# Two trunk layers on one core: five of 22 tile pairs of the FFN's up projection by Strassen's scheme, and another place for the down projection's Strassen part

## The chip, the core and the metric

The kernel is one program on one core of a Trainium2 chip. TensorE (PE) multiplies matrices, with a second list (PEld) for loading the weights of the next matmul; VectorE (DVE) and ScalarE (ACT) do elementwise work and empty the accumulators; GpSimd (POOL) does little here; SyncE (SP) issues the DMAs. The metric is the device time of one execution in microseconds (us), lower is better, told as the median of several runs.

## The reference, cut to what matters

T = 528 tokens (16 learned meta tokens and 512 frames) of width 1024 go through two layers, each a mixer and a gated feed-forward net. Only the second half of a layer and the projection ahead of it matter here:

```python
for l in range(DEPTH):                       # DEPTH = 2
    h = h + hybrid_mixer(rms_norm(h, norm_mix[l]), ...)    # its last step: y @ w_out, 1024 x 1024
    n = rms_norm(h, norm_ffn[l])
    gate, up = split(n @ w_up[l], 2)         # w_up: 1024 x 5632, so 2816 columns each
    gate = causal_dwconv(gate, conv_ffn[l])  # per column, three tokens wide
    h = h + (silu(gate) * up) @ w_down[l]    # w_down: 2816 x 1024
return h[:, N_META:]
```

## The kernel before, in words

**Layout and precision.** Tokens lie on the free axis and features on the partitions, so an activation is a row of tiles of 128 features by 528 tokens, and a weight tile of 128x128 is what TensorE holds still while tokens stream through. Every fp32 product is made of three matmuls in the format float32r: each operand is a high part (its rounded copy) and a low part (the rest), and high·high, high·low and low·high add up in one PSUM accumulator. `stage()` (L230) loads a raw weight tile of up to 128x512, four inner tiles side by side, by a DMA on SP's queue into one of four buffers `wst`; `two()` (L235) makes `wh` (ScalarE, L241) and `wl` (VectorE, L242) of it, three buffers each. A raw tile is free again when its `wl` is there, a split tile when its matmuls are done. `spans()` (L245) cuts the tokens in two halves of 264; in the second layer, where the meta tokens' outputs are not needed, a gate tile has halves of 256 and 258 tokens and an up tile one stretch of 512. `denses()` (L252, matmul L267) makes output tiles over all inner tiles; `dense()` (L274) is the same for one tile.

**PSUM** has eight banks, in four pools of two, with the tags a, g, s and x.

**w_out** (loop at L982) makes four pairs of output tiles. For each tile VectorE adds the result to the residual (L993), SP stores `hk` to DRAM, and `Norm.feed` (L183) multiplies by the norm's gain and leaves X, high by ScalarE (L186) and low by VectorE (L187), and the running sum of squares. The norm's factor for each token, `rb`, is ready only a while later, so w_up works on X without it and multiplies its results by rb instead.

**w_up** (`ffn()`, loop at L1010) goes over 22 feature tiles j; each is a pair of output tiles, gate and up. The gate tile has banks "g" and "a" in turn (L1014), the up tile "s" and "a" (L1032). VectorE multiplies the gate halves by rb into `cs` (L1023); the convolution is one ScalarE step (L1026) and two VectorE steps (L1028) in `cv`; tanh (L1030) and L1031 give twice the silu; the up halves become `uu` (L1035), and L1036 multiplies both. The result F is split into high (ScalarE, L1063) and low (VectorE, L1064) for w_down. For the first eight j, `parts()` (L1042 to L1061) instead forms the operands of a Strassen scheme, of two neighbouring feature tiles and two token halves: four blocks in the tile's own buffer, three more in `far`, a buffer with the tag "ar".

**w_down** (loop at L1074) makes four pairs of output tiles. A pair of output tiles, two inner tiles and two token halves are a 2x2 block product, which in Winograd's form of Strassen's scheme takes seven block products in place of eight. Each output pair begins with this for the first eight feature tiles: raw tiles (L1097), sums of weight blocks `s12` and `s34` on VectorE (L1106 to L1109), and the products (matmul L1091). Two products share a bank X1 or X2 (tag x) with others, so the sums P1, U2, U3, U4 of products are taken in between (L1125, L1138 to L1144). Then the other 14 feature tiles follow in chunks of four (L1146), with `addto` (L1134) adding the Strassen sums to the residual after the first of them.

**Order.** The program is written in the order above; the Tile framework's scheduler sets the order of the instructions on each engine by it, with the splits and weight sums raised to the front (`tc.high_priority(HI)`), and inserts the semaphores.

## Time and profile before

| | |
|---|---|
| runs, us | 1706.68, 1707.40, 1707.92; median 1707.4 |
| profiled execution, us | 1708.38, its span 1706.5 |
| granted TensorE clock | 0.999 |
| DMA | 173.78 MB, 102 GB/s over the span |
| w_out, layer 0 / layer 1 | 437.0 to 485.4 / 1290.0 to 1337.8 |
| w_up, layer 0 / layer 1 (without its first gate tile) | 493.5 to 740.1 / 1345.6 to 1583.6 |
| w_down, layer 0 / layer 1 | 740.1 to 864.7 / 1583.6 to 1706 |

The stages are stretches of the one profiled execution, in us from the span's start, cut where TensorE goes over to the next. In the views, "busy" is an engine's time at work, "x" a count of instructions, a line like `L242 DVE TENSOR_TENSOR wl<-wst,wh` an operation by its place in the code with the tiles that it writes and reads, and "<-" behind a wait the engine and instruction that ended it. A granted clock of 1.00 is full speed.

### The profile page before, as it was taken

The numbers are of one execution on the slowest core, as the hardware profiler recorded it, in microseconds if no ns is written. First come the engines' busy times: TensorE is split into PE (matmuls) and PEld (weight loads), VectorE is DVE, ScalarE is ACT, GpSimd is POOL, SyncE is SP. The second block draws the span as 40 slices with busy tenths as digits, with TensorE's granted clock in tenths as the row PEclk, the third lists the DMA queues.
The fourth block names the chain that finished last, engine by engine and source line by source line (L and its number), as shares of the span: only waits on it lengthen the run. The fifth ranks groups of instructions, "written<-read, shape, count | busy, mean of one in ns | idle before, by whom it ended". The sixth has DMA issues, their size and how long they took to land.

```text
span 1706.5 us, 34827 instructions
## 1 busy us (share of the span) xinstructions
PE 1695.2 (99%) x13476; PEld 1586.5 (93%) x13476; DVE 1281.4 (75%) x2998; ACT 777.8 (46%) x1697; POOL 75.2 (4%) x190
## 2 busy tenths in 40 slices
PE   9999999999999999999999999999999999999999
PEld 8899888889999999999998999888899999999888
DVE  6899999866667766666558998998666677666654
ACT  6553566653444433334335535566634444333332
POOL 1000111100000000000000000110000000000000
PEclk9999999999999999999999999999999999999999
DMA  6322211225533222234343122112265333333433
GB/s 206 99 63 87 76 51 46 83 72 178 173 116 90 93 88 93 89 108 144 117 141 99 62 88 81 51 45 80 70 180 175 113 94 96 93 93 95 130 118 100
DMA packets 95094, 173.78 MB, mean 102 GB/s; under 512 B 10704, under 2 KB 15536, under 8 KB 94672
## 3 DMA queue, kind: packets, MB, share of 16 engines
q1 hardware_dynamic: 93456, 167.01, 32.0%
q10 hardware_dynamic: 1472, 4.54, 0.8%
q8 instruction: 106, 1.74, 0.4%
q14 instruction: 60, 0.49, 0.1%
HBM read 154.04 MB, written 17.06 MB: 100 GB/s over the span
## 4 chain that ended last, share of the span: by engine, by line
PE 91%; DVE 5%; ACT 2%; issue 1%; DMA 0%; ACTq 0%; DVEq 0%
PE a L267 62%; PE a L1091 13%; PE misc L303 2%; PE iq L303 2%; PE vps L740 1%; PE oBT L903 1%; PE isc L486 1%; PE tps L751 1%; PE logit L879 1%; DVE wl L242 1%; PE PTp L897 1%; PE dS L794 0%; ACT ar L789 0%; ACT junk L656 0%; DVE va L777 0%
## 5 line engine op out<-in xcount | busy, mean ns | idle before, releaser
L267 PE MATMUL a<-X,wh 128*128 128x264 f32 (+4 forms) x4768 | 947.4, 295 | 0.0
L267 PEld LDWEIGHTS a<-X,wh 128*128 128x128 f32 x4768 | 755.1, 188 | 20.3 <-issue 0.2
L267 PE MATMUL a<-X,wl 128*128 128x264 f32 (+4 forms) x2384 | 701.2, 294 | 0.0
L241 ACT ACTIVATE wh<-wst 128x512 fp32r<-128x512 f32 (+2 forms) x512 | 313.7, 613 | 603.2 <-PE a L267 329.4
L242 DVE TENSOR_TENSOR wl<-wst,wh 128x512 fp32r<-128x512 f32 (+2 forms) x512 | 341.7, 668 | 178.9 <-ACT wh L241 163.3
L267 PEld LDWEIGHTS a<-X,wl 128*128 128x128 f32 x2384 | 450.0, 189 | 10.9
L1091 PE MATMUL a<-F,wh 128*128 128x264 f32 (+2 forms) x984 | 202.5, 303 | 0.0
L1091 PEld LDWEIGHTS a<-F,wh 128*128 128x128 f32 x984 | 157.7, 188 | 7.8
L1091 PE MATMUL a<-F,wl 128*128 128x264 f32 (+2 forms) x492 | 149.0, 303 | 0.6 <-DVE wl L242 0.6
L1091 PEld LDWEIGHTS a<-F,wl 128*128 128x128 f32 x492 | 92.6, 188 | 4.8 <-DVE wl L242 1.0
L267 PE MATMUL a<-Y,wh 128*128 128x264 f32 (+2 forms) x512 | 92.9, 283 | 0.0
L267 PEld LDWEIGHTS a<-Y,wh 128*128 128x128 f32 x512 | 79.1, 188 | 0.0
L267 PE MATMUL a<-Y,wl 128*128 128x264 f32 (+2 forms) x256 | 72.5, 283 | 0.0
L1028 DVE SCALAR_TENSOR_TENSOR cv<-cs,vec,cv 128x528 f32<-128x528 f32 (+1 forms) x88 | 67.0, 761 | 3.1 <-ACT cv L1026 1.1
L1023 DVE TENSOR_TENSOR cs<-a,rb 128x264 f32<-128x264 f32 (+1 forms) x88 | 37.4, 427 | 38.8 <-PE a L267 35.8
L1035 DVE TENSOR_TENSOR uu<-a,rb 128x264 f32<-128x264 f32 (+1 forms) x66 | 33.9, 516 | 32.6 <-PE a L267 32.6
L361 DVE SCALAR_TENSOR_TENSOR cv<-cs,vec,cv 128x528 f32<-128x528 f32 x72 | 54.3, 756 | 0.9 <-ACT cv L359 0.8
L844 DVE MAX8 m<-ar 128x8 f32<-128x256 f32 (+2 forms) x96 | 53.1, 553 | 1.1
L845 DVE MATCH_REPLACE8 ar<-m,ar 128x256 f32<-128x256 f32 (+2 forms) x96 | 51.8, 540 | 0.0
L267 PEld LDWEIGHTS a<-Y,wl 128*128 128x128 f32 x256 | 48.2, 188 | 0.0
L1030 ACT ACTIVATE th<-cv 128x528 f32<-128x528 f32 (+1 forms) x44 | 27.8, 633 | 31.8 <-DVE cv L1028 31.7
L1031 DVE SCALAR_TENSOR_TENSOR cv<-th,cv 128x528 f32<-128x528 f32 (+1 forms) x44 | 30.7, 698 | 13.8 <-ACT th L1030 13.7
(352 smaller groups left out, 2458.0 us busy)
## 6 DMA issues: line engine op xcount, KB each, us to landing
wst<-w_up SPq DMA_DIRECT2D x176, 256.0 KB, 2.7
wst<-w_down SPq DMA_DIRECT2D x80, 256.0 KB, 2.7
wst<-w_a SPq DMA_DIRECT2D x64, 256.0 KB, 2.7
wst<-w_gate SPq DMA_DIRECT2D x64, 256.0 KB, 2.9
wst<-w_out SPq DMA_DIRECT2D x32, 256.0 KB, 2.9
hk<-h SPq DMA_DIRECT2D x24, 264.0 KB, 3.4
tg<-gg SPq DMA_DIRECT2D x16, 264.0 KB, 2.3
gr<-tg SPq DMA_DIRECT2D x16, 264.0 KB, 2.7
```

The source lines that it names most:

```text
L241: S.activation(h, w, AF.Copy)
L242: V.tensor_tensor(lo, w, h.bitcast(F32), op=sub)
L267: mms.append(PE.matmul(ps[j][:, :t.stop - t.start], w[:, ws], x[:, t], start=(kk == 0 and w is h and part == 0), stop=(kk == kts - 1 and w ...
L303: mms.append(PE.matmul(b[:, c:], X[kk][:, part, o:o + 128], w[:, c:], start=(kk == 0 and w is h and part == 0), stop=(kk == KT - 1 and w i ...
L361: V.scalar_tensor_tensor(cv, cs[:, i:i + T], vc(cw + i), cv, op0=mul, op1=add)
L844: V.max(m8, sc)
L845: V.match_replace(sc, m8, sc, SEL)
L1023: V.tensor_tensor(cs[:, 2 + t.start:2 + t.stop], p, rb[:, t], op=mul)
L1028: V.scalar_tensor_tensor(cv[:, t0:], cs[:, t0 + i:i + T], vec[:, cw + i:cw + i + 1], cv[:, t0:], op0=mul, op1=add)
L1031: V.scalar_tensor_tensor(cv[:, t0:], th[:, t0:], 1.0, cv[:, t0:], op0=add, op1=mul)
L1035: V.tensor_tensor(uu[:, t], p, rb[:, t], op=mul)
L1091: PE.matmul(o, c(ww), r, start=first, stop=fin and ww is w[1], skip_group_check=True)
```

## The change

Three things change.

- **w_up.** For the five feature tiles j in `UP` the gate tile and the up tile are made together, by the scheme that w_down uses: the two output tiles, neighbouring inner tiles and two token halves as blocks, over the whole inner dimension of eight tiles. `up7()` does it. The scheme itself is the new function `seven()` (L277 of the changed kernel), which both projections call. A pair has two raw tiles for each half of the inner dimension, hence all four `wst` buffers, eight weight sums in `wsum`, and 84 matmuls (L284) of half the tokens. The three steps one, mid and end add up the products in `cs` and `uu`, and the multiplications by rb follow there as two instructions of the full width. The remaining 17 pairs stay as they were.
- **w_out.** What the scheme needs of X beside its blocks (T1 to T4, high and low) is formed behind each pair of output tiles, by six VectorE instructions of half the tokens and one of all, and ScalarE's high parts. Three of the four sets lie in the buffer "ar", the fourth in the buffer of feature tiles 20 and 21.
- **w_down.** The Strassen scheme now takes the last eight feature tiles in place of the first eight, so that `far` is filled after w_up's use of "ar" is over. For the first output pair the three plain chunks of four come first, then Strassen, then the addition to the residual and the last chunk of two; the other output pairs begin with Strassen as before.

The number of matmuls stays the same, and their columns fall from 3,268,590 to 3,237,990. The diff, cut to its core (w_down's old lines, which do the same as `seven()`, are left out):

```diff
@@ -27,6 +27,7 @@
 SP = 4
 INV = -2e38
+UP = (2, 5, 8, 11, 14)
@@ -273,6 +274,49 @@
+    def seven(src, ks, ops, sums, X1, X2, C0, C1, C2, first, steps):
+        def mm3(o, st, w, c, x):
+            for ww, part in ((w[0], 0), (w[0], 1), (w[1], 0)):
+                PE.matmul(o, ww[:, c:c + 128], x[:, part], start=st, stop=False, skip_group_check=True)
+                st = False
+        def run(jobs, w, i, stride, off):
+            for o, res, name, blk in jobs:
+                for q in range(2):
+                    mm3(o, first(res) if i == 0 and q == 0 else False, w, off * blk + stride * q, ops[2 * i + q][name])
+        raw, ss, wa = [], [], []
+        for k in ks:
+            r = [stage(src[u][:, k * 128:k * 128 + 512], 512).rearrange("p (q c) -> p q c", q=2) for u in range(2)]
+            raw.append(r)
+            wa.append(two(r[0].rearrange("p q c -> p (q c)"), 512))
+        for i, r in enumerate(raw):
+            t12, t34 = [t.rearrange("p (a q c) -> p a q c", a=2, q=2) for t in sums(i)]
+            A = [r[i // 2][:, :, 128 * (i % 2):128 * (i % 2) + 128] for i in range(4)]
+            with tc.high_priority(HI):
+                V.tensor_tensor(t12[:, 0], A[2], A[3], op=add)
+                V.tensor_tensor(t34[:, 0], A[0], A[2], op=sub)
+                V.tensor_tensor(t12[:, 1], t12[:, 0], A[0], op=sub)
+                V.tensor_tensor(t34[:, 1], A[1], t12[:, 1], op=sub)
+            ss.append([t.rearrange("p a q c -> p (a q c)") for t in (t12, t34)])
+        n = range(len(ks))
+        for i in n:
+            run([(X1, "X1", "B11", 0), (C0, 0, "B21", 1)], wa[i], i, 256, 128)
+        steps[0]()
+        for i in n:
+            w = [t.rearrange("p q c -> p (q c)") for t in two(raw[i][1][:, :, 128:], 256)]
+            run([(C2, 2, "T4", 0)], w, i, 128, 0)
+        for i in n:
+            run([(X2, "X2", "T2", 1), (X1, "X1", "T1", 0)], two(ss[i][0], 512), i, 128, 256)
+        steps[1]()
+        for i in n:
+            run([(C1, 1, "B22", 1), (X2, None, "T3", 0)], two(ss[i][1], 512), i, 128, 256)
+        steps[2]()
@@ -979,6 +1023,11 @@
+        nh = (T - t0 + 3) // 4 * 2
+        s1, s2 = slice(t0, t0 + nh), slice(T - nh, T)
+        xar = p1.tile([128, AR], F32R, tag="ar", name="xar")
+        xq = None
+        nf.ops = []
@@ -995,6 +1044,29 @@
+            i = m0 // 2
+            if i == 3:
+                xq = Q(10, [128, 2112], F32R, name="xq")
+            tv = (xq if i == 3 else xar[:, 8 * nh * i:])[:, :8 * nh].rearrange("p (a b t) -> p a b t", a=4, b=2)
+            e, o = hks
+            ge, go = [gains[:, nf.off + m0 + u:nf.off + m0 + u + 1] for u in range(2)]
+            td = p2.tile([128, T], F32, tag="cv", name="td", bufs=2)
+            tt = p2.tile([128, T + 3], F32, tag="cs", name="tt", bufs=2)
+            d, f, t3, t2 = td[:, :nh], td[:, nh:2 * nh], tt[:, :nh], tt[:, nh:2 * nh]
+            S.activation(f, e[:, s2], AF.Copy, scale=ge)
+            V.tensor_tensor(d, e[:, s2], e[:, s1], op=sub)
+            V.scalar_tensor_tensor(t3, o[:, s2], go, f, op0=mul, op1=sub)
+            V.scalar_tensor_tensor(t2, e[:, s1], ge, t3, op0=mul, op1=add)
+            S.activation(tv[:, 0, 0], d, AF.Copy, scale=ge)
+            V.scalar_tensor_tensor(tv[:, 0, 1], d, ge, tv[:, 0, 0].bitcast(F32), op0=mul, op1=sub)
+            V.scalar_tensor_tensor(f, o[:, s1], go, t2, op0=mul, op1=sub)
+            for k, x in ((slice(1, 3), tt[:, :2 * nh].rearrange("p (a t) -> p a t", a=2)), (slice(3, 4), f[:, None])):
+                S.activation(tv[:, k, 0], x, AF.Copy)
+                V.tensor_tensor(tv[:, k, 1], x, tv[:, k, 0].bitcast(F32), op=sub)
+            xe, xo = nf.x[m0:m0 + 2]
+            nf.ops.append(dict(B11=xe[:, :, s1], B21=xo[:, :, s1], B22=xo[:, :, s2],
+                               T1=tv[:, 0], T3=tv[:, 1], T2=tv[:, 2], T4=tv[:, 3]))
@@ -1006,12 +1078,45 @@
-        far = p1.tile([128, AR], F32R, tag="ar", name="far")
+        mh = (T - t0 + 3) // 4 * 2
+        z1, z2 = slice(t0, t0 + mh), slice(T - mh, T)
+        J0 = FT - 2 * SP
+        def up7(j, cs, uu):
+            g = "ga"[j % 2]
+            b0, b1 = [sm([128, mh], "a", g) for _ in range(2)]
+            b2 = sm([128, mh], "a", "s")
+            X1, X2 = [sm([128, mh], "a", "x") for _ in range(2)]
+            pu = p1.tile([128, 1024], F32, tag="ikT", name="pu")
+            P1, U2, U3 = [pu[:, mh * i:mh * i + mh] for i in range(3)]
+            sq = p1.tile([128, 2112], F32, tag="Q9", name="wsum")
+            c1, c2 = [cs[:, 2 + z.start:2 + z.stop] for z in (z1, z2)]
+            def one():
+                S.activation(P1, X1, AF.Copy)
+                V.tensor_tensor(c1, b0, P1, op=add)
+            def mid():
+                V.tensor_tensor(U2, X2, P1, op=add)
+                V.tensor_tensor(c2, X1, U2, op=add)
+            def end():
+                V.tensor_tensor(U3, X2, P1, op=add)
+                V.tensor_tensor(c2, c2, b1, op=add)
+                V.tensor_tensor(uu[:, z1], b2, U3, op=add)
+                V.tensor_tensor(uu[:, z2], X1, U3, op=add)
+            seven([a["w_up"][l, 2 * j + u] for u in range(2)], (0, 4), nf.ops,
+                  lambda i: [sq[:, 1024 * i + 512 * u:1024 * i + 512 * u + 512] for u in range(2)],
+                  X1, X2, b0, b1, b2, lambda i: True if i is not None else False, (one, mid, end))
         for j in range(FT):
+            if j == J0:
+                far = p1.tile([128, AR], F32R, tag="ar", name="far")
 ...
-            ps = dense(a["w_up"][l, 2 * j], KT, lambda k, part: X[k][:, part], t0, "ga"[j % 2])
+            ps = None if j in UP else dense(a["w_up"][l, 2 * j], KT, lambda k, part: X[k][:, part], t0, "ga"[j % 2])
 ...
-            for p, t in ps:
-                V.tensor_tensor(cs[:, 2 + t.start:2 + t.stop], p, rb[:, t], op=mul)
+            if j in UP:
+                uu = p2.tile([128, T], F32, tag="hk", name="uu", bufs=2)
+                up7(j, cs, uu)
+                V.tensor_tensor(cs[:, 2 + t0:2 + T], cs[:, 2 + t0:2 + T], rb[:, t0:], op=mul)
+            else:
+                for p, t in ps:
+                    V.tensor_tensor(cs[:, 2 + t.start:2 + t.stop], p, rb[:, t], op=mul)
 ...
-            ps = pu0 if j == 0 else dense(a["w_up"][l, 2 * j + 1], KT, lambda k, part: X[k][:, part], t1, "sa"[j % 2])
-            uu = p2.tile([128, T], F32, tag="hk", name="uu", bufs=2)
-            for p, t in ps:
-                V.tensor_tensor(uu[:, t], p, rb[:, t], op=mul)
+            if j in UP:
+                V.tensor_tensor(uu[:, t1:], uu[:, t1:], rb[:, t1:], op=mul)
+            else:
+                ps = pu0 if j == 0 else dense(a["w_up"][l, 2 * j + 1], KT, lambda k, part: X[k][:, part], t1, "sa"[j % 2])
+                uu = p2.tile([128, T], F32, tag="hk", name="uu", bufs=2)
+                for p, t in ps:
+                    V.tensor_tensor(uu[:, t], p, rb[:, t], op=mul)
             V.tensor_tensor(uu[:, t1:], uu[:, t1:], cv[:, t1:], op=mul)
-            if j < 2 * SP:
+            if j >= J0:
                 ys = yt[:, :8 * nh].rearrange("p (a b t) -> p a b t", a=4, b=2)
-                ye = far[:, 6 * nh * (j // 2):6 * nh * (j // 2 + 1)].rearrange("p (a b t) -> p a b t", a=3, b=2)
+                ye = far[:, 6 * nh * ((j - J0) // 2):6 * nh * ((j - J0) // 2 + 1)].rearrange("p (a b t) -> p a b t", a=3, b=2)
 ...
+            def strassen():
+                tt = p2.tile([128, T], F32, tag="th", name="ts", bufs=2)
+                tu = p2.tile([128, T], F32, tag="th", name="tu", bufs=2)
+                P1, U2, U3, U4 = tt[:, :nh], tt[:, nh:2 * nh], tu[:, :nh], tu[:, nh:2 * nh]
+                def one():
+                    S.activation(P1, X1, AF.Copy)
+                def mid():
+                    V.tensor_tensor(U2, X2, P1, op=add)
+                    V.tensor_tensor(U4, X1, U2, op=add)
+                def end():
+                    V.tensor_tensor(U3, X2, P1, op=add)
+                    V.tensor_tensor(U2, X1, U3, op=add)
+                def sums(i):
+                    return (p2.tile([128, T + 3], F32, tag="cs", name="s12", bufs=2)[:, :512],
+                            p2.tile([128, T], F32, tag="cv", name="s34", bufs=2)[:, :512])
+                seven(src, range(J0, FT, 4), S7, sums, X1, X2, C[0], C[1], C[2], first, (one, mid, end))
+                return P1, U4, U3, U2
+            def others(k0):
+                kn = min(WC, J0 - k0)
                 for u in range(2):
                     w = weights(src[u][:, k0 * 128:(k0 + kn) * 128], kn * 128)
+                    for h in range(1 if wide else 2):
+                        o = cb[u][:, :2 * nh] if wide else C[2 * u + h]
+                        t = slice(t1, T) if wide else (s1, s2)[h]
                         for k in range(kn):
+                            for ww, part in ((w[0], 0), (w[0], 1), (w[1], 0)):
+                                PE.matmul(o, ww[:, 128 * k:128 * k + 128], Yf[k0 + k][:, part, t],
+                                          start=first(2 * u + h) if k == 0 and part == 0 and ww is w[0] else False,
+                                          stop=False, skip_group_check=True)
+            ks = list(range(0, J0, WC))
+            n = len(ks) - 1 if m0 == 0 else 0
+            for k0 in ks[:n]:
+                others(k0)
```

More of the change, by code (lines that the diff above doesn't have):

```diff
@@ L1084, in ffn @@
             C = [cb[i // 2][:, nh * (i % 2):nh * (i % 2 + 1)] if wide else cb[i][:, :nh] for i in range(4)]
-            new = [True] * 4
             X1, X2 = [sm([128, nh], "a", "x") for _ in range(2)]
-            def mm3(o, first, w, c, x, t=None, fin=False):
-                for ww, part in ((w[0], 0), (w[0], 1), (w[1], 0)):
-                    r = x[:, part] if t is None else x[:, part, t]
-                    PE.matmul(o, c(ww), r, start=first, stop=fin and ww is w[1], skip_group_check=True)
-                    first = False
@@ L1095, in ffn @@
-            pairs = range(0, SP, 2)
-            raw, s12, s34, wa = [], [], [], []
-            for p0 in pairs:
-                r = [stage(src[u][:, p0 * 256:p0 * 256 + 512], 512).rearrange("p (q c) -> p q c", q=2) for u in range(2)]
-                raw.append(r)
-                wa.append(two(r[0].rearrange("p q c -> p (q c)"), 512))
-            for r in raw:
-                t12 = p2.tile([128, T + 3], F32, tag="cs", name="s12", bufs=2)[:, :512].rearrange("p (a q c) -> p a q c", a=2, q=2)
-                t34 = p2.tile([128, T], F32, tag="cv", name="s34", bufs=2)[:, :512].rearrange("p (a q c) -> p a q c", a=2, q=2)
-                A = [r[i // 2][:, :, 128 * (i % 2):128 * (i % 2) + 128] for i in range(4)]
-                with tc.high_priority(HI):
-                    V.tensor_tensor(t12[:, 0], A[2], A[3], op=add)
-                    V.tensor_tensor(t34[:, 0], A[0], A[2], op=sub)
-                    V.tensor_tensor(t12[:, 1], t12[:, 0], A[0], op=sub)
-                    V.tensor_tensor(t34[:, 1], A[1], t12[:, 1], op=sub)
-                s12.append(t12.rearrange("p a q c -> p (a q c)"))
-                s34.append(t34.rearrange("p a q c -> p (a q c)"))
@@ L1112, in ffn @@
-            cols = lambda o: (lambda w: w[:, o:o + 128])
-            def run(jobs, w, p0, i, stride, off):
-                for o, first, name, blk in jobs:
-                    for q in range(2):
-                        mm3(o, first and i == 0 and q == 0, w, cols(off * blk + stride * q), S7[p0 + q][name])
-            for i, p0 in enumerate(pairs):
-                run([(X1, True, "B11", 0), (C[0], True, "B21", 1)], wa[i], p0, i, 256, 128)
-            tt = p2.tile([128, T], F32, tag="th", name="ts", bufs=2)
@@ L1123, in ffn @@
-            tu = p2.tile([128, T], F32, tag="th", name="tu", bufs=2)
-            P1, U2, U3, U4 = tt[:, :nh], tt[:, nh:2 * nh], tu[:, :nh], tu[:, nh:2 * nh]
-            S.activation(P1, X1, AF.Copy)
-            for i, p0 in enumerate(pairs):
-                w = two(raw[i][1][:, :, 128:], 256)
-                w = [t.rearrange("p q c -> p (q c)") for t in w]
-                run([(C[2], True, "T4", 0)], w, p0, i, 128, 0)
-            for i, p0 in enumerate(pairs):
-                w = two(s12[i], 512)
-                run([(X2, True, "T2", 1), (X1, True, "T1", 0)], w, p0, i, 128, 256)
+            begun = set()
@@ L1134, in addto, with first @@
+            def first(i):
+                if i is None or i in ("X1", "X2"):
+                    return i is not None
+                b = i // 2 if wide else i
+                r = b not in begun
+                begun.add(b)
+                return r
             def addto(i, x):
@@ L1136, in addto @@
                 V.scalar_tensor_tensor(d, x, 0.5, d, op0=mul, op1=add)
-            V.tensor_tensor(U2, X2, P1, op=add)
-            V.tensor_tensor(U4, X1, U2, op=add)
-            for i, p0 in enumerate(pairs):
-                w = two(s34[i], 512)
-                run([(C[1], not wide, "B22", 1), (X2, False, "T3", 0)], w, p0, i, 128, 256)
-            V.tensor_tensor(U3, X2, P1, op=add)
-            V.tensor_tensor(U2, X1, U3, op=add)
-            for k0 in range(2 * SP, FT, WC):
-                if k0 == 2 * SP + WC:
-                    for i, x in enumerate((P1, U4, U3, U2)):
-                        addto(i, x)
-                kn = min(WC, FT - k0)
+            def strassen():
[15 more added lines that the diff above has]
+                return P1, U4, U3, U2
@@ L1162, in ffn @@
+            ks = list(range(0, J0, WC))
+            n = len(ks) - 1 if m0 == 0 else 0
+            for k0 in ks[:n]:
+                others(k0)
+            us = strassen()
+            for i, k0 in enumerate(ks[n:]):
+                if i == 1 or m0 == 0:
+                    for c, x in enumerate(us):
+                        addto(c, x)
+                others(k0)
             for u in range(2):
```

8 lines of the change are left out of this document (removed).

## The prediction

> **What bounds the kernel now.** The page comes first, for the share of each engine and for the chain.
>
> ```profile
> span 1706.5 us, 34827 instructions
> ...
> PE 1695.2 (99%) x13476; PEld 1586.5 (93%) x13476; DVE 1281.4 (75%) x2998; ACT 777.8 (46%) x1697; POOL 75.2 (4%) x190
> ...
> PE 91%; DVE 5%; ACT 2%; issue 1%; DMA 0%; ACTq 0%; DVEq 0%
> ```
>
> TensorE is busy for 99% of the span and holds 91% of the chain, so time goes only where matmul columns go, and it comes back where TensorE starts to wait. Whether it can wait is read stage by stage, from the windows: w_out of layer 0, w_up of layer 0, four of its plain pairs of tiles, the second Strassen pair of w_down in layer 0, and w_up of layer 1.
>
> ```profile
> core 0: us, PE busy (x) PEld busy (x) DVE busy (x) ACT busy (x) POOL busy (x), PEclk, DMA share, GB/s
> 437.00:485.40 48.40, 48.40 (x400) 48.40 (x400) 27.87 (x48) 19.70 (x33) 0.00 (x0) 1.00 0.54 169
> 493.50:740.10 246.60, 246.60 (x2018) 246.60 (x2018) 180.05 (x313) 98.39 (x163) 1.99 (x20) 1.00 0.30 91
> 587.30:634.20 46.90, 46.90 (x386) 46.90 (x385) 31.56 (x52) 17.71 (x28) 0.40 (x4) 1.00 0.30 91
> 768.50:784.00 15.50, 15.40 (x126) 15.13 (x125) 13.94 (x30) 8.15 (x15) 0.00 (x0) 1.00 0.58 174
> 1345.60:1583.60 238.00, 238.00 (x1514) 215.65 (x1514) 173.50 (x291) 97.71 (x163) 1.99 (x20) 1.00 0.31 94
> ```
>
> In w_up TensorE has no gap; VectorE (DVE) is at 73% in both layers, ScalarE at 40%. The fourth row matters most: a Strassen pair with VectorE at 90% of the time, and TensorE still at 15.40 of 15.50 us. The waits view gives what TensorE loses to splits of weights in the whole program, three times in all, in w_down:
>
> ```profile
> PE a L1091 <- DVE wl L242: 1.2, 3, 0.6
> ```
>
> **The matmuls.** Layer 0: 246.60 us over 2018 matmuls of 264 columns is 122.2 ns each. A plain pair is 2 tiles x 8 inner tiles x 2 halves x 3 = 96; by Strassen it is 7 products x 4 x 3 = 84. So 12 x 122.2 ns = 1.47 us less a pair, 7.3 us for five. Layer 1: a plain pair is 48 matmuls of 256 or 258 columns and 24 of 512, 24,624 columns in all; the window holds 21 pairs, so 238.0 / 21 = 11.33 us a pair, 0.460 ns a column. After it, 84 x 258 = 21,672 columns, 9.97 us; 1.36 us less, taken at 1.34 because 258-column matmuls might cost a little more by the column, 6.7 us for five. Together **14.0 us**. The seven products are in the order of the changed program, so this much is certain to leave TensorE's list. The clock is 1.00 in every window.
>
> **What VectorE gets.** Its prices, layer 0, w_up:
>
> ```profile
> L242 DVE TENSOR_TENSOR wl<-wst,wh 128x512 fp32r<-128x512 f32 x84 | 57.9, 689 | 12.2 <-ACT wh L241 12.0
> L1028 DVE SCALAR_TENSOR_TENSOR cv<-cs,vec,cv 128x528 f32<-128x528 f32 x44 | 33.8, 769 | 1.5 <-ACT cv L1026 0.3
> L1023 DVE TENSOR_TENSOR cs<-a,rb 128x264 f32<-128x264 f32 x44 | 18.9, 431 | 19.8 <-PE a L267 19.4 <-ACT rb L221 0.2
> L1031 DVE SCALAR_TENSOR_TENSOR cv<-th,cv 128x528 f32<-128x528 f32 x22 | 15.6, 708 | 13.7 <-ACT th L1030 13.5
> L1036 DVE TENSOR_TENSOR uu<-uu,cv 128x528 f32<-128x528 f32 x21 | 14.7, 700 | 0.0
> L1106 DVE TENSOR_TENSOR s<-wst 128x256 f32<-128x256 f32 x2 | 0.8, 421 | 0.0
> ```
>
> A plain pair: 4 splits of 0.69, 4 evacuations of 0.43, two steps of 0.77, then 0.71, 0.70 and a last split of 0.70: 8.1 us (7.9 measured, 31.56 / 4). A Strassen pair: 6 splits of 0.69 and 2 of 0.42, 8 weight sums of 0.42, 7 steps on the products of 0.43, 2 multiplications by rb of 0.70, and the same 3.65 of convolution, gate and split: 16.4 us. Every third pair is a Strassen pair, so three pairs hold 32.7 us of VectorE against 2 x 11.73 + 10.27 = 33.7 us of TensorE. At these whole durations VectorE is nearly the bound. But they overlap:
>
> ```profile
> 506.38 0.70 DVE L1036 TENSOR_TENSOR uu<-uu,cv 128x528 f32<-128x528 f32 x1
> 507.12 0.43 DVE L1055 TENSOR_TENSOR uu<-uu 128x264 f32<-128x264 f32 x1
> ...
> 603.62 0.43 DVE L1023 TENSOR_TENSOR cs<-a,rb 128x264 f32<-128x264 f32 x1 [0.20 <-PE a L267]
> ...
> 768.54 0.42 DVE L1106 TENSOR_TENSOR s<-wst 128x256 f32<-128x256 f32 x1 [2.76 <-DMA wst<-w_down]
> 768.88 0.68 DVE L242 TENSOR_TENSOR wl<-wst,wh 128x512 fp32r<-128x512 f32 x1
> 769.48 0.42 DVE L1107 TENSOR_TENSOR s<-wst 128x256 f32<-128x256 f32 x1
> 769.82 0.42 DVE L1108 TENSOR_TENSOR s<-s,wst 128x256 f32<-128x256 f32 x1
> ```
>
> An instruction that doesn't read the one ahead starts 0.08 us before that one's end: 0.34 us after a start of 256 columns, 0.60 after one of 512 (so 0.35 for 264, 0.63 for 528, 0.68 for a 0.77 step). One that reads it starts 0.04 after the end (506.38 to 507.12). With that, a queue of VectorE work is a tenth shorter, some 30 us in three pairs. [...]
>
> **The tightest place.** VectorE's list at a plain pair, program before (names: cs, uu the evacuated tiles, wl the low split, F the operand for w_down):
>
> ```order
> L242 TENSOR_TENSOR wl<-wst,wh 128x512
> L1023 TENSOR_TENSOR cs<-a,rb 128x264 x2
> L242 TENSOR_TENSOR wl<-wst,wh 128x512
> L1028 SCALAR_TENSOR_TENSOR cv<-cs,vec_158,cv 128x528 x2
> L1031 SCALAR_TENSOR_TENSOR cv<-th,cv 128x528
> L242 TENSOR_TENSOR wl<-wst,wh 128x512
> L1035 TENSOR_TENSOR uu<-a,rb 128x264 x2
> L242 TENSOR_TENSOR wl<-wst,wh 128x512
> L1036 TENSOR_TENSOR uu<-uu,cv 128x528
> ```
>
> And after, where Strassen pair 11 begins while pair 10 is still being finished:
>
> ```order
> L305 TENSOR_TENSOR wsum<-wst,wsum 128x256
> L1138 SCALAR_TENSOR_TENSOR cv<-cs,vec_158,cv 128x528
> L243 TENSOR_TENSOR wl<-wst,wh 128x512
> L1148 TENSOR_TENSOR uu<-a,rb 128x264
> L1141 SCALAR_TENSOR_TENSOR cv<-th,cv 128x528
> L1148 TENSOR_TENSOR uu<-a,rb 128x264
> L243 TENSOR_TENSOR wl<-wst,wh 128x256
> L1149 TENSOR_TENSOR uu<-uu,cv 128x528
> L243 TENSOR_TENSOR wl<-wst,wh 128x256
> L1177 TENSOR_TENSOR F_7958<-uu,F_7958 128x528
> L1097 TENSOR_TENSOR cs<-a,pu 128x264
> L243 TENSOR_TENSOR wl<-wsum,wh 128x512 x4
> ```
>
> The first weight sum's split stands behind the whole end of the pair before it, and the four raw tiles take all four staging buffers. Their DMA and ScalarE's part:
>
> ```profile
> wst<-w_up SPq DMA_DIRECT2D x176, 256.0 KB, 2.7
> ```
>
> ```profile
> L241 ACT ACTIVATE wh<-wst 128x512 fp32r<-128x512 f32 x83 | 52.1, 628 | 85.5 <-PE a L267 51.9 <-issue 33.5
> ...
> L1063 ACT ACTIVATE F<-uu 128x528 fp32r<-128x528 f32 x13 | 8.4, 646 | 17.9 <-DVE uu L1036 17.9
> ```
>
> Zero is the pair's first matmul. The fourth raw tile's buffer comes free with the second split of pair 10's up tile, about -6.7; 2.7 us of DMA and the issue put it at -3.7. From there: three sums 1.10, a cv step 0.68, a sum 0.34, a cv step 0.77, a split 0.61, uu 0.35, the gate product 0.68, uu 0.35, a split of 256 0.34, product 0.63, split 0.34: +2.4. F waits for ScalarE (0.65), starts at 2.9 and takes 0.63; the evacuation of the first product 0.35; the split 0.61: **+4.5**. TensorE wants it at the third matmul after 36, 36 x 0.122 + 0.245 = 4.65. It fits by 0.15 us. The other nine pairs have the same list (layer 1 with 0.2). I take 0.1 us of wait a pair for scatter, 1.0 in all; the ends are 0 and 1.0 us each. Behind an even Strassen pair the next tile needs its gate banks back at 5.87 and 7.34 us after the pair; VectorE's list gets there at 5.6 and 7.1. At the first odd tile, pair 1 of layer 0, the sums of pair 2 push the second bank's evacuation to 9.9 us after that tile's start against 9.5: 0.4 us.
>
> **w_down.** Its work is the same, but in the first output pair Strassen now stands behind three chunks, and only 24 matmuls (2.9 us) part it from that of the second pair; before it was 168 (20.5 us). VectorE there, before (X the next layer's operands, s_ the sums):
>
> ```order
> L1109 TENSOR_TENSOR s_10009<-wst,s_10008 128x256
> L1136 SCALAR_TENSOR_TENSOR hk<-a,hk 128x264
> L242 TENSOR_TENSOR wl<-wst,wh 128x256
> L1136 SCALAR_TENSOR_TENSOR hk<-a,hk 128x264 x2
> L187 SCALAR_TENSOR_TENSOR X_9962<-hk,gains,X_9962 128x528
> L242 TENSOR_TENSOR wl<-wst,wh 128x256
> L187 SCALAR_TENSOR_TENSOR X_9970<-hk,gains,X_9970 128x528
> L242 TENSOR_TENSOR wl<-s_10002,wh 128x512
> ```
>
> and after:
>
> ```order
> L305 TENSOR_TENSOR s_10170<-wst,s_10169 128x256
> L1211 SCALAR_TENSOR_TENSOR hk<-ts,hk 128x264
> L1211 SCALAR_TENSOR_TENSOR hk<-a,hk 128x264
> L243 TENSOR_TENSOR wl<-wst,wh 128x256
> L1211 SCALAR_TENSOR_TENSOR hk<-a,hk 128x264 x3
> L188 SCALAR_TENSOR_TENSOR X_10121<-hk,gains,X_10121 128x528
> L243 TENSOR_TENSOR wl<-s_10163,wh 128x512
> ```
>
> The residual additions of the first pair's Strassen results have joined the queue ahead of the first sum's split. Walked as above it ends 5.3 us into the second pair's Strassen, against 4.65: 0.7, where before 768.50 to 784.00 lost 0.1 and the waits 0.6 at most; the first pair loses 0.3 at the step that frees its second product. I charge 1.1 us for both layers, with -0.4 (the old waits go) and 2.5 as ends.
>
> **w_out and the rest.** Forming the new operands adds, for each of four output pairs, six VectorE instructions of 264 (0.35) and one of 528 (0.63), 2.7 us, and 1.9 of ScalarE. In layer 0 VectorE goes from 27.87 to 38.8 of 48.4 us, 80%; the free fifth covers it, and the last X7 is ready at 3.3 us of the first gate tile, which wants it at 4.0. Without that cover 2.7 us would fall on the path; I take 0.5 for both layers (0 to 2). Moving w_down's operand work from the first eight feature tiles to the last eight moves a load that cost TensorE nothing.
>
> **Sum.** -14.0 + 1.0 + 0.4 + 1.1 + 0.5 = -11.0 us. The profiled execution took 1708.4 us (span 1706.5 and 1.9 around it), 1.0 above the median of the runs, 1707.4. So 1697.4 there, and **1696.4** for the median.
>
> **Rivals.**
> *Nothing waits* (0.14): the window with VectorE at 90% speaks for it, the margin of 0.15 us against it. -14.0: 1693.4.
> *VectorE pays whole durations* (0.15): the mechanism of the rule on draining. Then the list above ends at 5.4 to 6.0 instead of 4.5, 1.0 us of wait in each of ten pairs; the odd tile behind an even Strassen pair waits 0.6 for its bank (three a layer, 3.6), the odd tile ahead of one 1.05 (two a layer, 4.2), w_down 2.5: 20.3 - 14.0 = +6.3, 1713.7, slower. It decides from about 0.7 us a group of two tiles; against it stand the starts quoted above.
> *The fourth raw tile lands late* (0.13): four buffers, all held until the small splits; 3.6 us instead of 2.7 pushes the same list by 0.9 in each pair, 9 us on top of the forecast: 1705.4, no change. For it: 2.76 us of idle for just such a DMA in w_down; against it: w_up moves 91 GB/s where w_out moves 169.
> *The forecast* has 0.58.
>
> **Numbers.** 0.2%, 3.4 us, is about what can be told from no change here, so faster is below 1704.0. Faster: the first rival and most of the forecast, 0.69; same: the late tile and a forecast with double costs, 0.15; slower 0.16. The range runs from 1692.5 (nothing waits, and w_down's old waits go) to 1707.0 (the late tile, and a little more) and leaves out the draining rival.
>
> **What would show it.** In the profile after: w_up of layer 0 near 240 us and of layer 1 near 232; VectorE near 85% there; TensorE's waits for wl of the sums under 0.3 us each. Waits of about 1 us at all ten pairs, or w_up no shorter than before, would make the prediction wrong; so would a gap in w_out.

## The result and the profile after

The changed kernel takes **1697.13 us** in the median of four runs (1695.42 to 1698.31), the kernel before 1707.04 beside it: a ratio of 0.994, with a 95% interval of 0.9923 to 0.9958. The forecast was 1696.4 us. The profiled execution took 1696.78 us with a span of 1695.0, that is 11.5 less than the span of before, where the sum had said 11.0. The page of the changed kernel begins so:

```profile
span 1695.0 us, 35229 instructions
...
PE 1682.9 (99%) x13476; PEld 1579.7 (93%) x13476; DVE 1360.1 (80%) x3229; ACT 819.0 (48%) x1779; POOL 75.8 (4%) x190
...
PE 90%; DVE 6%; ACT 3%; issue 1%; DMA 0%; ACTq 0%; DVEq 0%
```

TensorE is as full as before over a shorter span, and VectorE has gone from 75% to 80%. Where the time went is read stage by stage, each stage cut at the first matmul of the next. First the windows of the kernel before: w_up and w_down of layer 0, w_up of layer 1.

```profile
479.43:739.97 260.54, 260.54 (x2135) 260.54 (x2133) 186.87 (x332) 102.86 (x169) 1.99 (x20) 1.00 0.30 92
739.97:864.56 124.59, 123.84 (x1010) 123.12 (x1009) 71.96 (x151) 44.55 (x82) 2.45 (x10) 1.00 0.41 121
1331.84:1583.43 251.59, 251.59 (x1607) 228.16 (x1606) 180.51 (x310) 102.07 (x169) 1.99 (x20) 1.00 0.31 95
```

And of the changed kernel (the columns as in the prediction): w_out and w_up of layer 0, three pairs of which one is by Strassen, w_down of layer 0, w_out and w_up of layer 1, and the rest to the end.

```profile
432.90:479.60 46.70, 46.70 (x386) 46.70 (x385) 35.79 (x69) 25.51 (x46) 0.10 (x1) 1.00 0.56 176
479.64:732.94 253.30, 253.30 (x2075) 253.11 (x2074) 213.32 (x413) 116.26 (x194) 2.47 (x23) 1.00 0.31 94
549.51:583.25 33.74, 33.74 (x279) 33.74 (x278) 29.32 (x57) 15.94 (x26) 0.30 (x3) 1.00 0.32 95
732.94:858.29 125.35, 124.29 (x1011) 123.27 (x1009) 76.78 (x163) 46.45 (x86) 5.08 (x10) 1.00 0.44 133
1279.50:1325.60 46.10, 46.10 (x387) 46.10 (x386) 35.22 (x70) 25.24 (x45) 0.10 (x1) 1.00 0.56 173
1325.60:1572.34 246.74, 246.10 (x1666) 227.43 (x1665) 208.31 (x396) 114.90 (x194) 2.11 (x21) 1.00 0.32 96
1572.34:1695.00 122.66, 119.11 (x757) 107.35 (x755) 69.17 (x144) 38.91 (x69) 0.00 (x0) 1.00 0.40 118
```

| stage, us | before | after | measured | forecast |
|---|---|---|---|---|
| up to w_out, layer 0 (not touched) | 432.68 | 432.89 | +0.21 | 0 |
| w_out, both layers | 92.85 | 92.86 | +0.01 | +0.5 |
| w_up, layer 0 | 260.54 | 253.30 | **-7.24** | -7.3 + 0.5 + 0.4 |
| w_up, layer 1 | 251.59 | 246.74 | **-4.85** | -6.7 + 0.5 |
| w_down, layer 0 | 124.59 | 125.35 | +0.76 | +1.1 for both layers |
| w_down, layer 1, to the end | 123.07 | 122.66 | -0.41 | |
| mixer, layer 1 (not touched) | 421.18 | 421.20 | +0.02 | 0 |

The seven rows add up to -11.50 us. What TensorE still waits for, by the waits view of the changed kernel:

```profile
PE a L284 <- DVE wl L243: 1.0, 3, 0.4
...
PE a L268 <- DVE cs L1133: 0.6, 3, 0.2
```

The first row is w_down's, three times in layer 0; none of the 40 splits of weight sums in w_up's ten Strassen pairs appears. The second is new, all three times in w_up of layer 1, and is the piece that the prediction did not have.

### The profile page after: what moved, and what is told of

Its sections match the earlier page's. It is cut to its first block, busy times and chain, and to the rows that moved or that the text cites. A ratio compares the mean times of both kernels' runs of the same rounds, so it can differ in the third digit from the quotient of the medians.

```text
span 1695.0 us, 35229 instructions
## 1 busy us (share of the span) xinstructions
PE 1682.9 (99%) x13476; PEld 1579.7 (93%) x13476; DVE 1360.1 (80%) x3229; ACT 819.0 (48%) x1779; POOL 75.8 (4%) x190
## 4 chain that ended last, share of the span: by engine, by line
PE 90%; DVE 6%; ACT 3%; issue 1%; DMA 0%; ACTq 0%; DVEq 0%
PE a L268 55%; PE a L284 10%; PE a L1245 9%; PE misc L347 2%; PE iq L347 2%; PE vps L784 2%; PE oBT L947 1%; PE isc L530 1%; PE tps L795 1%; DVE wl L243 1%; PE logit L923 1%; PE PTp L941 1%; PE dS L838 1%; ACT ar L833 0%; ACT wh L242 0%
## 5 line engine op out<-in xcount | busy, mean ns | idle before, releaser
L268 PE MATMUL a<-X,wh 128*128 128x264 f32 (+4 forms) x4208 | 837.1, 295 | 0.6 <-DVE cs L1133 0.6
L268 PEld LDWEIGHTS a<-X,wh 128*128 128x128 f32 x4208 | 666.9, 189 | 17.7 <-issue 1.4
L268 PE MATMUL a<-X,wl 128*128 128x264 f32 (+4 forms) x2104 | 618.4, 294 | 0.0
L268 PEld LDWEIGHTS a<-X,wl 128*128 128x128 f32 x2104 | 397.9, 189 | 9.1
L1245 PE MATMUL a<-F,wh 128*128 128x264 f32 (+2 forms) x728 | 154.8, 309 | 0.0
L1245 PEld LDWEIGHTS a<-F,wh 128*128 128x128 f32 x728 | 118.0, 188 | 7.3
L1245 PE MATMUL a<-F,wl 128*128 128x264 f32 (+2 forms) x364 | 112.7, 310 | 0.0
L268 PE MATMUL a<-Y,wh 128*128 128x264 f32 (+2 forms) x512 | 92.9, 283 | 0.0
L268 PEld LDWEIGHTS a<-Y,wh 128*128 128x128 f32 x512 | 79.1, 188 | 0.0
L268 PE MATMUL a<-Y,wl 128*128 128x264 f32 (+2 forms) x256 | 72.5, 283 | 0.0
L268 PEld LDWEIGHTS a<-Y,wl 128*128 128x128 f32 x256 | 48.2, 188 | 0.0
L284 PE MATMUL a<-F,wh 128*128 128x264 f32 (+1 forms) x256 | 47.9, 284 | 0.0
L284 PE MATMUL a<-xar,wh 128*128 128x264 f32 (+1 forms) x240 | 45.6, 283 | 0.0
L284 PE MATMUL a<-X,wh 128*128 128x264 f32 (+1 forms) x240 | 44.8, 283 | 0.0
```

The source lines that it names most:

```text
L268: mms.append(PE.matmul(ps[j][:, :t.stop - t.start], w[:, ws], x[:, t], start=(kk == 0 and w is h and part == 0), stop=(kk == kts - 1 and w ...
L284: PE.matmul(o, ww[:, c:c + 128], x[:, part], start=st, stop=False, skip_group_check=True)
L1245: PE.matmul(o, ww[:, 128 * k:128 * k + 128], Yf[k0 + k][:, part, t], start=first(2 * u + h) if k == 0 and part == 0 and ww is w[0] else False,
```

## The experiments

Times are medians; the kernel before ran beside them at 1707.58, 1707.39 and 1707.69 us (in the order of the groups e1 to e4, e5 to e8, e9 to e11). The intervals of two versions often overlap, so versions are set against each other by the stage times of their profiles, which repeat: w_out of layer 0 took 46.75 or 46.76 us in all 13 profiles.

**What the side edits cost: e1 and e8.** In e1 the list of Strassen pairs is empty:

```diff
-UP = (2, 5, 8, 11, 14)
+UP = ()
```

> UP is empty: w_up is as before the change, w_out still forms the new operands (nothing reads them), w_down has its Strassen part at the last eight feature tiles. Theory (the stage times of the two traces: w_out 46.72 to 46.70 us and 46.06 to 46.10, w_down 124.59 to 125.35 in layer 0 and 119.54 to 118.94 from first to last matmul in layer 1): the two side edits cost 0.2 us together, so 1707.2 us beside 1707.0 of before, w_out 46.7 and 46.1 us. Rival (the prediction's own charges, 1.1 for w_down and 0.5 for w_out): 1708.6 us, with a gap on TensorE in w_out or right behind it.

Measured: 1709.32 us, ratio 1.001 (1.0001 to 1.0019). The stages: w_out 46.75 and 46.10, w_up 260.53 and 251.59, w_down 125.49 in layer 0 and 118.93 (first to last matmul) in layer 1, against 124.59 and 119.54. So the stages give +0.3 us, near the theory's 0.2, and there is no gap in w_out, which the rival had; yet the median is 1.7 higher, nearer the rival's number. In e8 the operands in w_out are gone as well:

```diff
-            i = m0 // 2
...
-            nf.ops.append(dict(B11=xe[:, :, s1], B21=xo[:, :, s1], B22=xo[:, :, s2],
-                               T1=tv[:, 0], T3=tv[:, 1], T2=tv[:, 2], T4=tv[:, 3]))
```

> The kernel before with the change to w_down alone: no Strassen pair in w_up and no new operands in w_out. Theory (stage times): w_down 0.8 us longer in layer 0 and 0.6 shorter in layer 1: 0.2 us more than before. With the operands as well the median was 1.7 us more than before (interval 0.2 to 3.2) while the stages from w_out on showed 0.3. If the operands cost the rest, this run is 0.2 above before and the other 1.7; if w_down does, both are 1.7 above; if neither stage shows it here either, the rest lies in stages that no edit touches.

Measured: 1708.88 us, ratio 1.0008 (0.9999 to 1.0017), w_down 125.26 and 119.16 us: +0.3. The operands cost nothing, and the rest is in neither edited stage. In both profiled executions w_out begins 1.7 to 2.0 us later than in that of before, and on the way there lies a short dip of the granted clock, to which the last section comes. The dip alone does not account for it: the changed kernel's profile has the same dip, and its w_out begins 0.2 us later; e3's has none, and its w_out begins 1.3 later. What makes up the medians was not shown.

**w_down's order: e6 and e7.** In e6 the first output pair begins with Strassen, in e7 two chunks come ahead of it and one follows:

```diff
-            n = len(ks) - 1 if m0 == 0 else 0
+            n = 0 if m0 == 0 else 0            # e6
+            n = 2 if m0 == 0 else 0            # e7
...
-                if i == 1 or m0 == 0:
+                if i == (0 if n else 1):
```

> The changed kernel, but w_down's first output pair begins with Strassen as the other three do, and the plain chunks follow. Theory: its operands of feature tiles 20 and 21 are formed by some 12 VectorE and ScalarE instructions behind the last matmul of w_up, and TensorE waits for them about 2 us in each layer: 1701 us, with a wait for F or far at the start of w_down. Rival: the matmuls of tiles 14 to 19 come first and hide it: 1697 us, and the 0.4 us that the second output pair lost (769.17 us) are back as well: 1696.5.

Measured: 1697.25 us, ratio 0.9942 (0.9928 to 0.9955). w_down took 125.29 and 119.58 us, and TensorE's only wait near its start is 0.18 us. The theory of a 2 us wait is wrong: the matmuls of the earlier tiles come first. The second output pair's wait is gone, as the rival had it, but the first pair loses about as much in small delays, and the stage is no shorter.

> The changed kernel, but in w_down's first output pair two plain chunks come ahead of Strassen and one more behind it, so that 72 matmuls (8.8 us) stand between its Strassen and the second pair's, in place of 24 (2.9 us). Theory (the prediction's step for w_down): the residual additions are off the queue by then, and the wait of 0.59 us at the second pair's first weight sum in layer 0 falls to the 0.27 of before; w_down of layer 0 125.0 us in place of 125.35, the time 1696.8 us. Rival: the wait is that of any pair behind another (0.46 to 0.49 at the third and fourth): 0.1 us at most, and the place costs nothing.

Measured: 1694.83 us, ratio 0.9931 (0.9915 to 0.9946). w_down of layer 0 took 124.82 us, 0.5 less than in the changed kernel (125.0 was expected), and that of layer 1 119.43, 0.5 more: there a split of a plain chunk is late by 0.59 us at 1610.86, as it was in the kernel before (0.56 at 1624.31). So the place of the first pair's Strassen part is worth half a microsecond in each layer, with opposite signs. The theory's reason did not hold, though: the wait at the second pair's first sum was to fall to 0.27 us, and it stayed (see w_down in the next section). The rest of this median's distance lies elsewhere: the mixer of layer 1 took 420.04 us in this profile.

**How much VectorE can take: e4, e2, e5, e11.** e4 adds four repeated sums (0.34 us each) to each Strassen pair of w_up (`extra` is 4 there; `i` is 0 and 1, the two halves of the inner dimension):

```diff
                 V.tensor_tensor(t34[:, 1], A[1], t12[:, 1], op=sub)
+                for _ in range(extra * i):
+                    V.tensor_tensor(t34[:, 1], A[1], t12[:, 1], op=sub)
...
-... (one, mid, end))
+... (one, mid, end), extra=4)
```

> The changed kernel with four more VectorE instructions of 256 columns (0.34 us each, 1.36 together) behind the weight sums of every Strassen pair of w_up; they repeat the last sum and change no result. Theory A (the prediction's tightest place): the split of the first weight sum ends 0.3 us ahead of the matmul that wants it, so 1.36 us more ahead of it makes TensorE wait 1.05 us in each of ten pairs, 10.5 us: 1707.6 us. Theory B (only the load counts, and the order of the list is made anew around the added work): 29.32 + 1.36 = 30.7 us of VectorE in 33.74 for three pairs is no bound, so under 1 us more: 1697 to 1698 us.

Measured: 1696.55 us, ratio 0.9936 (0.9923 to 0.995); w_up 254.83 and 246.67 us against 253.30 and 246.74. The 13.6 us of added VectorE work cost 1.5, not 10.5, which is far nearer to theory B (under 1) than to A. What A describes is seen in four of the ten pairs, the last four of layer 0: there the first sum's split still stands behind the gate product and the split of F, ends 4.86 us into the pair instead of 4.42, and is read 0.28 us later, 1.1 us in all. Only 0.44 of the added 1.36 us reach that split; idle places of VectorE ahead of it, such as 0.42 us before 608.78 in the changed kernel, took up much of the rest. In the other six pairs the new list has the first sum's split ahead of the split of F, in two of them ahead of the gate product too, and TensorE waits little or not at all for it. A margin counted on one list says little of another.

e2 has seven pairs:

```diff
-UP = (2, 5, 8, 11, 14)
+UP = (2, 4, 6, 8, 10, 12, 14)
```

> UP = (2, 4, 6, 8, 10, 12, 14): every second pair. Theory (VectorE's list overlaps): in the changed kernel three pairs, one of them by Strassen, hold 29.32 us of VectorE in 33.74; a plain pair before held 7.9, so a Strassen pair holds 13.5, and two pairs 21.4 of 21.98 us in layer 0 and 21.1 of 21.4 in layer 1. VectorE fits by 0.3 to 0.6 us: the matmuls give 7 x 1.47 + 7 x 1.245 = 19.0 us, and waits of up to 0.6 us at each of 14 pairs take at most 8.4 back: 1688 to 1697 us. Rival (VectorE pays whole durations): 16.4 + 8.1 = 24.5 us against 21.98, 2.5 us of wait in every two pairs, 35 in all: 1723 us, with VectorE the longest chain in w_up.

Measured: 1704.18 us, ratio 0.9981 (0.9971 to 0.999), between the two. Two pairs took 23.0 us, where 24.5 was the rival's least, but 21.98 the theory's. The timeline of TensorE in e2 shows what neither named:

```profile
545.20 0.75 PE L284 MATMUL a<-X,wh 128*128 128x264 f32 x4 [0.65 <-ACT wh L242]
545.82 0.51 PE L268 MATMUL a<-X,wh 128*128 128x264 f32 x2
```

and that of ScalarE:

```profile
544.51 0.63 ACT L242 ACTIVATE wh<-wst 128x512 fp32r<-128x512 f32 x1 [2.31 <-PE a L268]
```

L284 is the next Strassen pair, L268 the plain up tile around it: the scheduler has put four Strassen matmuls into it; with another bank for the up tile (e5) its order has none there. Their high split (544.51) waits 2.31 us for one of the three `wh` buffers, and TensorE then waits for that split. (This profile also has a dip of the granted clock in w_up of layer 0, near 571 us, which the last section shows; the 23.0 us are counted ahead of it, from 545.20 to 568.20.)

e3 is the changed kernel with another bank for the up tile behind an even Strassen pair:

```diff
-... t1, "sa"[j % 2])
+... t1, "s" if j - 1 in UP else "sa"[j % 2])
```

> The changed kernel, but the up tile that follows an even Strassen pair (j = 3, 9, 15) has banks of the tag s in place of a, so that it needs no bank of its own gate tile. Theory: the three waits of 0.37 us in layer 1 (for the evacuation of the gate's first half, at 1366.75, 1432.71 and 1498.68 us) are a matter of the bank alone and go: 1.1 us less, 1696.0 us, w_up of layer 1 245.6 us in place of 246.74. Rival: VectorE's queue is late there in any case, and TensorE waits as long at the next thing that it needs of VectorE (a split of weights or the next bank): 1697.1 us.

Measured: 1695.70 us, ratio 0.9931 (0.9919 to 0.9944). The three waits are gone, and w_up of layer 1 is 1.36 us shorter:

```profile
1325.38:1570.76 245.38, 245.38 (x1666) 227.28 (x1665) 208.09 (x396) 114.63 (x194) 2.09 (x21) 1.00 0.32 96
```

The wait was the bank's alone, and nothing took its place in w_up. e5 puts both edits together:

```diff
+UP = (2, 4, 6, 8, 10, 12, 14)
+... t1, "s" if j - 1 in UP else "sa"[j % 2])
```

> Seven Strassen pairs, UP = (2, 4, 6, 8, 10, 12, 14), and the up tile behind each of them in banks of the tag s, as in the two runs with one of these edits. With seven pairs alone TensorE waited 0.65 us twelve times for ScalarE's wh, at places where four matmuls of the next Strassen pair had been put into the middle of a plain up tile; with the other bank the order has no such place. Theory: that order was the loss, and VectorE's 13.5 + 7.9 = 21.4 us fit into 21.98: 7 x 1.47 + 7 x 1.245 = 19.0 us less than before but 0.2 for w_down: 1688 to 1690 us, w_up 250.3 us in layer 0 and 242.9 in layer 1. Rival: VectorE at 97% of the time is the bound and TensorE waits about 1 us in every two tiles wherever the matmuls stand: 1702 us or more.

Measured: 1695.73 us, ratio 0.9936 (0.9923 to 0.9948), w_up in both layers and two pairs of layer 0:

```profile
479.83:733.78 253.95, 252.80 (x2051) 250.69 (x2049) 223.86 (x447) 118.06 (x204) 2.46 (x23) 1.00 0.31 94
601.55:623.87 22.32, 22.25 (x181) 22.04 (x181) 21.27 (x44) 10.95 (x19) 0.20 (x2) 1.00 0.30 93
1325.57:1569.47 243.90, 243.46 (x1691) 227.12 (x1690) 217.94 (x432) 116.92 (x204) 2.10 (x21) 1.00 0.33 97
```

Half right. The 0.65 us waits were the order's and went. But layer 0 gives 6.6 us instead of 10.3: two pairs take 22.32 us instead of 21.98, with VectorE at 95%, and TensorE is late by 0.2 to 0.5 us at splits, those of the first sums above all. In layer 1 7.7 of 8.7 us remain. w_down, too, lost 1.7 us against the changed kernel, over both layers together (125.80 and 120.22 us).

e11 is a kernel with seven pairs in both layers and e3's bank, and takes VectorE's multiplication of `uu` by rb to GpSimd:

```diff
-                V.tensor_tensor(uu[:, t1:], uu[:, t1:], rb[:, t1:], op=mul)
+                G.tensor_tensor(uu[:, t1:], uu[:, t1:], rb[:, t1:], op=mul)
```

> Seven Strassen pairs in both layers with the bank s and the same w_down, and the multiplication of uu by rb (528 columns, 0.62 us of VectorE's time in each Strassen pair) on GpSimd, which is busy for 4% of the span. Theory (VectorE's time is what seven pairs lack in layer 0, 21.4 us in 21.98): 20.8 us fit, the late splits go, w_up 250.5 us in layer 0 and 243.0 in layer 1, 5.0 us less than the changed kernel: 1691 to 1692 us. Rival: GpSimd's multiplication, by its rows of 0.65 to 0.79 us for 256 columns some 1.5 us, comes late for the gate product or makes VectorE's instructions longer while it runs, and the waits stay: 1695 us or more.

Measured: 1700.86 us, ratio 0.9957 (0.9943 to 0.9972), w_up 257.19 and 246.39 us: worse by 3.2 and 2.5 than with seven pairs on VectorE. The timeline of GpSimd in e11:

```profile
610.98 1.34 POOL L1143 TENSOR_TENSOR uu<-uu,rb 128x528 f32<-128x528 f32 x1 [11.57 <-DVE uu L1107]
```

and of VectorE at the same time:

```profile
611.20 1.39 DVE L302 TENSOR_TENSOR wsum<-wst 128x256 f32<-128x256 f32 x1 [0.37 <-DMA wst<-w_up]
612.52 0.41 DVE L303 TENSOR_TENSOR wsum<-wst 128x256 f32<-128x256 f32 x1
```

A weight sum, of a kind that takes 0.41 us a moment later, takes 1.39 and ends 0.27 us after GpSimd: here VectorE pays 1.0 us to save 0.62. In w_up of layer 0 the 14 first sums (L302) took 10.0 us, against 5.9 in e5. (The list was also laid out anew around the moved step; how much of the loss is the order's was not tried.) The Trainium skill, page "SBUF — State Buffer", section "SBUF: two separate sides", says that a VectorE instruction with two SBUF inputs and a GpSimd instruction that reads SBUF take one port pair in turn, for a whole instruction each; the trace agrees.

**A version that is faster: e9 and e10.** Six pairs in layer 0 and seven in layer 1, with e3's bank, and w_down as in e7 in layer 0 and as in the changed kernel in layer 1 (e11 has that w_down too); e10 has six in both layers:

```diff
-UP = (2, 5, 8, 11, 14)
+UP = ((2, 4, 7, 9, 12, 14), (2, 4, 6, 8, 10, 12, 14))    # e9
+UP = ((2, 4, 7, 9, 12, 14), (2, 4, 7, 9, 12, 14))        # e10
...
-            n = len(ks) - 1 if m0 == 0 else 0
+            n = 2 + l if m0 == 0 else 0
```

> A version meant to beat both: six Strassen pairs in layer 0, j = 2, 4, 7, 9, 12, 14, and seven in layer 1, j = 2, 4, to 14; the up tile behind each in banks of the tag s; in w_down's first output pair two plain chunks ahead of Strassen in layer 0 and three in layer 1. Theory: in layer 0 only the pairs at a distance of two are late at the split of the first weight sum (0.6 us each, by the 3.7 us that seven pairs lost there), and the pair of three tiles that follows gives VectorE its time back, so w_up is 260.5 - 8.8 + 1.2 = 252.9 us at most and 251.7 at best; in layer 1 243.9; w_down 124.8 and 119.0 to 120.2: 3 to 4.5 us less than the changed kernel, 1692.6 to 1694.1 us. Rival: VectorE's load in layer 0 is the bound as soon as any two Strassen pairs stand at a distance of two: 253.9 us again and no gain over five pairs there, 1695 us or more.

Measured: **1692.42 us**, ratio 0.9911 (0.9896 to 0.9925), the lowest median of all, with both w_up stages:

```profile
479.74:732.71 252.97, 252.58 (x2063) 251.77 (x2062) 218.35 (x430) 117.19 (x199) 2.39 (x23) 1.00 0.31 94
...
1323.53:1566.55 243.02, 243.02 (x1691) 227.04 (x1690) 218.16 (x432) 116.78 (x204) 2.09 (x21) 1.00 0.32 97
```

Layer 1 has all that seven pairs can give (242.9) and makes 3.7 of the 4.7 us between the medians of e9 and the changed kernel. In layer 0 the sixth pair brings 0.33 of its 1.47 us, the theory's worst case.

> The same with six Strassen pairs in both layers, j = 2, 4, 7, 9, 12, 14. Theory: layer 1 has VectorE's list without lateness at six, so w_up there is 251.6 - 6 x 1.245 = 244.1 us, the same as with seven pairs and their 1.0 us of waits: the time is that of the version with seven within 0.3 us. Rival: 245.1 us, if the tiles at a distance of two cost their wait here too.

Measured: 1694.07 us, ratio 0.9918 (0.9904 to 0.9933), w_up of layer 1 244.14 us: 0.04 from the number expected for six. But the expectation that e9 and e10 take the same time within 0.3 us failed: they are 1.65 apart, since seven pairs did better in layer 1 than expected (243.02, not 243.9). By the stages its distance to e9 is the pair that layer 1 lacks (1.12) and a w_down of 0.2 and 0.6 us more.

## Why the prediction was right

The time was right to 0.7 us and the mechanism held: matmuls leave TensorE's list, and VectorE, at 87% in three pairs, lets them go. But part of the exactness is luck, since terms of opposite sign were off, and the reason given for w_down's term did not hold.

**The matmuls of layer 0, -7.3.** Right: -7.24 is measured with every wait counted in. Of the two charges on top, the one for the first odd tile came, at 0.25 us in place of 0.4 (two matmuls at 503.23 and 503.45 start 0.14 and 0.11 us late); for scatter (0.5) no late split is seen. That leaves 0.16 us of gain that no row accounts for.

**The matmuls of layer 1, -6.7.** Too high by 0.5, and the step that failed is the price of 0.460 ns a column, a mean over tiles of 256 to 512 columns. w_out of layer 1 has 384 matmuls of 256 or 258 columns in 46.10 us, 0.1200 each; 84 of them are 10.08 us, as the profile has each Strassen pair, not 9.97. A pair gains 1.25 and five 6.2. The trace of before has the same row of w_out, and it would have given the price:

```profile
1285.74:1331.84 46.10, 46.10 (x386) 46.10 (x385) 27.23 (x48) 19.02 (x31) 0.00 (x0) 1.00 0.57 173
```

**The tightest place.** Right, with a little more room than thought. The list of VectorE at pair 11 of layer 0:

```profile
609.31 0.71 DVE L1177 TENSOR_TENSOR F<-uu,F 128x528 fp32r<-128x528 f32 x1
609.94 0.43 DVE L1097 TENSOR_TENSOR cs<-a,pu 128x264 f32<-128x264 f32 x1
610.47 2.10 DVE L243 TENSOR_TENSOR wl<-wsum,wh 128x512 fp32r<-128x512 f32 x3
```

and TensorE's first matmul of the pair and the first that reads that split:

```profile
606.74 0.41 PE L284 MATMUL a<-X,wh 128*128 128x264 f32 x2
...
611.37 0.28 PE L284 MATMUL a<-xar,wl 128*128 128x264 f32 x1
```

The first split begins at 610.47 and takes 0.69 us (the 2.10 are three in a row), so it ends 4.42 us into the pair (4.34 at the forecast's 0.61 for a split), where 4.5 was forecast, and is read at 4.63. The rival that VectorE pays whole durations needs gaps that are not there:

```profile
617.21 0.43 DVE L1104 TENSOR_TENSOR pu<-a,pu 128x264 f32<-128x264 f32 x1
617.55 0.70 DVE L1130 TENSOR_TENSOR cs<-cs,rb 128x528 f32<-128x528 f32 x1
618.17 0.69 DVE L243 TENSOR_TENSOR wl<-wst,wh 128x512 fp32r<-128x512 f32 x1
618.77 0.43 DVE L1106 TENSOR_TENSOR uu<-a,pu 128x264 f32<-128x264 f32 x1
```

Three instructions of 0.43, 0.70 and 0.69 us take 1.56 from the first to the start of the fourth. The rule on draining, by which this rival goes, is that of the Trainium skill, page "VectorE: DVE Perf Modes", section "The DRAIN you can't avoid": the next instruction does not start until the pipe is empty. But the same section goes on to say that a next instruction that is not held (made to wait) starts earlier, and the trace agrees with that part: each of these starts 0.08 to 0.09 us before the end of the one ahead. So the page does not speak for the rival here. e4 says the same by the load: with 1.36 us more a pair the rival would have lost all of it.

**The bank behind an even Strassen pair.** In layer 0 the step held: the first half was evacuated by 5.47 us (forecast 5.6) against 5.87. It failed in layer 1, which was taken to be like it. The list of VectorE behind pair 8 of layer 1:

```profile
1430.94 0.69 DVE L1143 TENSOR_TENSOR uu<-uu,rb 128x512 f32<-128x512 f32 x1
1431.54 0.69 DVE L1141 SCALAR_TENSOR_TENSOR cv<-th,cv 128x514 f32<-128x514 f32 x1
1432.14 0.42 DVE L1133 TENSOR_TENSOR cs<-a,rb 128x256 f32<-128x256 f32 x1
```

and TensorE:

```profile
1432.22 0.28 PE L268 MATMUL a<-X,wl 128*128 128x258 f32 x1
...
1432.71 0.47 PE L268 MATMUL a<-X,wh 128*128 128x512 f32 x1 [0.21 <-DVE cs L1133]
```

There the up tile comes 48 x 0.12 = 5.76 us after the pair's end (1426.56), and the list has the multiplication L1143 and the gate step L1141 ahead of the evacuation, which ends 6.0 us after it. From one matmul's start to the next it is 0.49 us in place of 0.12. Three such places make the second missing piece; e3 measures it at 1.36 us. So layer 1 is -6.2 + 1.36 = -4.9.

**w_down, +1.1.** In layer 0 the places of the loss were right: from one matmul's start to the next the second output pair's first sum is 0.54 us late (0.26 before), the first pair loses 0.3, and the stage 0.76. The reason given for the first of these was not: the forecast blamed the additions of the first pair's Strassen results in VectorE's queue, and in e7, where they are no longer in it, that sum is still 0.49 late. In the changed kernel and in e7:

```profile
769.17 0.39 PE L284 MATMUL a<-far,wl 128*128 128x264 f32 x1 [0.38 <-DVE wl L243]
...
768.19 0.39 PE L284 MATMUL a<-far,wl 128*128 128x264 f32 x1 [0.33 <-DVE wl L243]
```

Most of what e7 wins in layer 0 is the first pair's loss; what makes the second pair's sum late there stays open. In layer 1 the old wait at 1624.31 went, as the lower end of the bounds had it, and gave 0.4 to 0.6 back. None of the places tried alike in both layers has the low time of both; e9, with two chunks first in layer 0 and three in layer 1, has (124.76 and 119.04 us), but e10 with the same w_down took 124.97 and 119.60.

**w_out, +0.5.** Nothing: VectorE was at 35.79 of 46.70 us, and the cover held.

**The late fourth tile.** In the changed kernel's w_up no weight sum waits for a DMA; the waits of that kind (8.9 us on VectorE, seven times) are w_down's, off TensorE's path.

Together: the charges that on balance did not come (0.5 and 0.4 in layer 0, 0.5 for scatter in layer 1, 0.5 for w_out, 0.75 for w_down) are 2.65 us, the pieces that were missing (0.5 of matmul price, 1.36 of bank) 1.86. The change of the median, -9.9 us, stands below the -11.5 of the profiled pair, because the latter compares an execution 1.3 us over its median with one 0.35 under its own.

## What to carry to other kernels

When one engine's list is shortened and another is to keep pace, walk the second engine's queue up to the instruction that the first waits for, at each distinct shape of the work: the same code with other halves had another order and another deadline, and only that one lost time. Take the price of a matmul from a row with that very shape. Where one more unit of the faster scheme would fit by the load, look at the banks and buffers that the scheduler has to cross to place it: here the bank decided more than VectorE's load did.
